# Down-projection weights of a float32 SwiGLU trunk: the low half comes from an accumulating transfer instead of a subtraction

## The chip, the cores and the metric

The kernel runs on one core of a Trainium2 chip. The metric is device time in microseconds (us), the median of several executions; lower is better.

## The reference

The program is a two-layer decoder trunk on 512 tokens of 1024 features, in float32. Layer 0 has a causal pooling mixer, layer 1 a latent attention; each mixer stands between two half-step SwiGLU feed-forward networks (FFNs), so there are four FFNs. The change touches the last product of each FFN alone:

```python
D_MODEL, SEQ, D_FF, FFN_HALF = 1024, 512, 2816, 0.5

def swiglu(h, w_gate, w_up, w_down):
    return (jax.nn.silu(h @ w_gate) * (h @ w_up)) @ w_down
...
        h = rmsnorm(x, ffn1_norm[i])
        x = x + FFN_HALF * swiglu(h, ffn1_w_gate[i], ffn1_w_up[i], ffn1_w_down[i])
```

## The kernel before

TensorE (PE in the rows) does its products in a float32 form with a short mantissa (float32r). To keep float32 precision, every operand is split into a high and a low half, `hi + lo = value`, and each product takes three matmuls in `mm3`: high by high, high by low, low by high. Only the last of the three reads the weights' low half.

Activations are kept with features in the 128 partitions and the 512 tokens along the free axis. Weights come from HBM tile by tile. `load_w` allocates three buffers of 128 x 1024 from the pool `wp`: `raw`, `whi` and `wlo`, each a ring of three. SyncE's queue (SP) loads `raw`; ScalarE (ACT) writes `whi`, a copy rounded to float32r; VectorE (DVE) writes `wlo = raw - whi`. These two are `split`, lines 117 and 118. TensorE then reads both.

An FFN has 22 blocks of 128 hidden features. They are worked off in three parts, `THIRDS`, of 8, 8 and 6 blocks. In each part the gate and up products are made (by `product` and by the seven-product scheme in `Two`), SiLU and the product with the up half follow (`gated`, lines 287 and 291), and the result is split into halves. Then the part's share of the down projection is made: eight tiles of weights, m = 0 to 7, one for each 128 output features. A tile of the first two parts has 1024 columns, and of the third 768; it takes 24 or 18 matmuls of 512 columns. VectorE adds half of the result to the residual (line 479). In the third part, each finished residual tile is at once prepared for the next layer on ScalarE and VectorE (`nxt.add`: lines 120, 121, 178, 181, 182).

The order of instructions on each engine isn't that of the program text. The language's planner orders them by its own costs, so weights of the first down tiles are split before the last gate and up results are done. What the rings allow still binds: the halves of tile m + 3 can only be written when TensorE is through with tile m, because both lie in the same buffers of `whi` and `wlo`.

GpSimd (POOL) has no work in the FFNs. It works in the two mixers (lines 182, 494, 834, 838, 937, 946).

Of the kernel before, what the change touches and what calls it, by code (L numbers as in the profile page):

```python
# [53 lines left out]
def _bits(v, n):  # L54
    """v cut to n significant bits (float64)."""
    m, e = np.frexp(v)
    return float(np.ldexp(np.trunc(np.ldexp(m, n)), e - n))
# [12 lines left out]
def _wrapped(v):  # L70
    """v less the nearest multiple of 2 pi, for an integer v, in extended precision."""
    pi2 = np.longdouble("6.283185307179586476925286766559005768")
    v = np.longdouble(v)
    return float(v - np.rint(v / pi2) * pi2)
# [3 lines left out]
def trunk(ctx: ExitStack, tc: tile.TileContext, a: dict, out: bass.AP):  # L78
# [29 lines left out]
    def mm3(ps, w, x, first, last):  # L108
        """w, x: (hi, lo) pairs; the product's three parts, in one group."""
        mm(ps, w[0], x[0], first, False)  # L110
        mm(ps, w[0], x[1], False, False)
        mm(ps, w[1], x[0], False, last)

    def split(src, hi, lo, scale=None):
        """hi + lo = src * scale exactly as float32, each with 12 bits."""
        if scale is None:
            nc.scalar.activation(hi, src, AF.Copy)  # L117
            nc.vector.tensor_tensor(out=lo, in0=src, in1=hi.bitcast(F32), op=ALU.subtract)  # L118
        else:
            nc.scalar.activation(hi, src, AF.Copy, scale=scale)  # L120
            nc.vector.scalar_tensor_tensor(  # L121
                out=lo, in0=src, scalar=scale, in1=hi.bitcast(F32), op0=ALU.mult, op1=ALU.subtract
            )
# [8 lines left out]

    # ---- x, constants
    gains = cp.tile([P, NG], F32, name="gains")
# [4 lines left out]
    nc.vector.memset(ones, 1.0)  # L139
    # the copy's table, ahead of its use  # L140
    nc.scalar.activation(small(1, tag="mx", bufs=6), ones[:, 0:1], AF.Copy)

    # ---- 1/sqrt on [P, n]
    def rsqrt(v, n, out=None):
# [18 lines left out]

    # ---- x_j: its gained halves for the next layer, and its share of the sum of squares
    class Prep:
# [23 lines left out]
        def rstd(self):  # L189
            """[P, NT]: token t of tile i in partition t, column i."""  # L190
            ps = aux()
            for i in range(NT):
                mm(ps[:, i : i + 1], self.sq[:, i * P : (i + 1) * P], ones[:, 0:1], True, True)
            v = small(NT, tag="ms")
            nc.vector.tensor_scalar(v, ps[:, :NT], 1.0 / D, EPS, op0=ALU.mult, op1=ALU.add)
            return rsqrt(v, NT, tp.tile([P, NT], F32, tag="rstd", name="rstd", bufs=2))

        def rstd_rows(self, r):
            """[P, S]: the same in every partition, tokens along the free axis."""
            ps = aux()  # L200
# [8 lines left out]
    def opening(wg, wu, prep):  # L209
        """the first tile of gate and up, as x and the weights come in."""  # L210
        half = WC // 2
# [46 lines left out]
    def ffn_in(fp, wg, wu, wd, prep, nxt, first, final):  # L258
# [5 lines left out]
        def product(w, x, turned=False, then=None):  # L264
            """then, if given, comes before the last steps"""
            hi, lo = load_w(w, WC)
# [16 lines left out]
        def gated(zg, zu):  # L283
            """silu(zg) * zu in halves; zg in parts, the last in the tile that is written."""
            z = zg[-1][1]
# [9 lines left out]

        # The first tiles take x unscaled, and their products are scaled by the tokens' 1/rms.
        # The others take xn, x scaled first, and most of them the gate's tiles two at a time,
        # by seven products of halves (Winograd's form of Strassen's): xn in blocks of 512
        # features by 256 tokens, the weights in blocks of 512 features by 128 columns.
        # Tokens of one size keep these sums as good as float32's own.  # L300
        xn, ts, kept = [None] * KD, {}, []
# [4 lines left out]
        def normed(k):  # L306
            """tiles k and KH + k of xn in halves; both stay in float32 as well."""
            tag, dt = (("s", F32), ("s", F32), ("chi", F32R), ("clo", F32R))[k]
# [12 lines left out]
        def x_sums(k):  # L321
            """the four sums of xn's blocks, a (hi, lo) pair for each tile of 128 features."""
            b11, b12, b21, b22 = (kept[k][:, c * C : (c + 1) * C] for c in range(4))
# [11 lines left out]
        def w_sums(top, low):  # L335
            """the blocks of two weight tiles, and their four sums, as (hi, lo) pairs."""
            hw = WC // 2
# [26 lines left out]
        class Two:  # L364
            """two tiles of columns by seven products, in two steps"""

# [17 lines left out]
            def end(self):  # L384
                """for each tile the parts it lies in; all but the first are in one tile"""
                p, q, u, za, zb = self.p, self.q, self.u, self.za, self.zb
# [25 lines left out]
        for f0, f1 in THIRDS:  # L412
# [55 lines left out]
            for m in range(KD):  # L468
                hi, lo = load_w(wd[m][:, f0 * P : f1 * P], nf * P)
                # the last tile of all leaves in two parts  # L470
                nc_ = 2 if final and f1 == NFT and m == KD - 1 else 1
# [16 lines left out]
    def pool_layer(prep, nxt):  # L488
        """x += scale * (window mean - token) @ w, tokens pooled by a banded product."""
        with tc.tile_pool(name="pp", bufs=1) as pp:  # L490
# [37 lines left out]
            def pools(q, m):  # L528
# [3 lines left out]
                for i in range(NT):  # L532
                    # 256 columns at a time: the band's own, then or before it zeros
                    at = min(i, 2) * P
# [34 lines left out]

    # ---- rotary tables [P, NT, 64], tokens in partitions; gains taken in  # L570
    tabs = {}
# [81 lines left out]
    def mla_layer(prep, nxt):  # L653
        with tc.tile_pool(name="mp", bufs=1) as mp:
# [21 lines left out]
            def latent(m):  # L676
                """features in partitions, gained but not yet scaled by their rms."""
                hi, lo = load_w(a["w_in"][m], WC)
# [18 lines left out]

            # shared rotary key
            raw = wp.tile([P, WC], F32, tag="raw", name="raw")
# [5 lines left out]
            )  # L705
            # high parts give the first 64 rows, low parts the others
            pk = acc()
# [16 lines left out]
            def rotated(dst, src, tab, heads):  # L724
                """src, dst: [P, NT, heads, 64] views, may be the same."""
                t1, t2 = tab
# [26 lines left out]
            def latent_rms(e, n):  # L753
                """r / rms of a latent, and its square."""
                ps = aux()
# [12 lines left out]
            for m in range(KQ):  # L768
                latent(m)
            # the exponential's table, ahead of its use  # L770
            nc.scalar.activation(small(1, tag="mx", bufs=6), gqk, AF.Exp)
# [8 lines left out]

            # Generators that yield the matmuls they issued, in columns of 512, so that
            # one head's attention can be cut into another pair's projections.
            def rsqrt_of(ss, f2, more=None):
                """1 / rms over a head, from sums of squares [P, NT, 2] and their scale."""
                v = tp.tile([P, NT, 2], F32, tag="v8", name="v8", bufs=2)
# [9 lines left out]
            def project(c, got):  # L795
                """heads 2c, 2c + 1: q, k, v with tokens in partitions; q unscaled, k and v scaled."""
                qsb = mp.tile([P, NT, 2, DN + DR], F32, tag="qsb", name="qsb", bufs=2)
# [8 lines left out]
                for i in range(NT):  # L806
# [18 lines left out]
                    yield 6.0  # L825
                # k's head norm, taken into k
                y = rsqrt_of(ss[:, 1], be2, skp)
# [43 lines left out]

                # q's rotary part, and its head norm for the scores' rows
                qpe = mp.tile([P, NT, 2, 2, DR], F32, tag="qpe", name="qpe")
# [10 lines left out]
            class Head:  # L884
                """one head's attention in steps; o, features in partitions, as (hi, lo)."""

# [11 lines left out]
                def turn_rot(self):  # L898
                    """[hi; lo] of q against k's hi and lo, each twice over."""
                    h = self.h  # L900
# [41 lines left out]
                def turn_p(self, half):  # L942
                    """P transposed: blocks of 128 keys by 256 queries, two to a slot."""
                    pts = [[slot([P, 2, 2 * P]) for _ in range(half + 1)] for _ in range(2)]
# [45 lines left out]

            # steps of the heads in turn, other products between them
            n = H // 2
# [76 lines left out]

# ---- layout on the host  # L1070


def _cols(v):
    """[n * P] -> [P, n]."""
    return v.reshape(-1, P).T


def _lhs(w):
    """[.., K, M] -> [.., M / P, P, K] : tile m, row p of each K block, K block by column."""
    *b, k, m = w.shape  # L1080
# [73 lines left out]
```

## Time and profile before

| | |
|---|---|
| time of the kernel before, 3 runs | 1698.12, 1699.06 (median), 1699.32 us |
| profiled execution: span from first to last instruction | 1697.1 us |
| TensorE busy in the span | 1683.8 us |
| VectorE busy | 1076.1 us |
| ScalarE busy | 702.3 us |
| GpSimd busy | 70.1 us |
| loads of the down projection | 64 of 512 KB and 32 of 384 KB |

The profiled execution has no run time of its own beside the span; the median of the three runs is 2.0 us above the span, which is what lies before the first and after the last instruction. TensorE's busy time counts an instruction from its first column in to its last column out, and these overlap from one matmul to the next; a pause of TensorE shows only where even the overlap is gone.

### The profile page before, as it was taken

The numbers are of one execution on the slowest core, as the hardware profiler recorded it, in microseconds if no ns is written. First come the engines' busy times: TensorE is split into PE (matmuls) and PEld (weight loads), VectorE is DVE, ScalarE is ACT, GpSimd is POOL, SyncE is SP. The second block draws the span as 40 slices with busy tenths as digits, with TensorE's granted clock in tenths as the row PEclk, the third lists the DMA queues.
The fourth block names the chain that finished last, engine by engine and source line by source line (L and its number), as shares of the span: only waits on it lengthen the run. The fifth ranks groups of instructions, "written<-read, shape, count | busy, mean of one in ns | idle before, by whom it ended". The sixth has DMA issues, their size and how long they took to land.

```text
span 1697.1 us, 23211 instructions
## 1 busy us (share of the span) xinstructions
PE 1683.8 (99%) x9238; PEld 1462.2 (86%) x9238; DVE 1076.1 (63%) x1824; ACT 702.3 (41%) x1163; POOL 70.1 (4%) x147
## 2 busy tenths in 40 slices
PE   8999999999999999999999999999999999999999
PEld 7888988887888988888889889888888789898897
DVE  8845645698845545569556455646778796465463
ACT  6423423364423423444324223546665453243241
POOL 0000000012000000000000000003321300000000
PEclk9999999999999999999999999999999999999999
DMA  5333332232322332332323323321112123233232
GB/s 176 97 109 97 104 98 97 87 114 76 111 92 95 106 98 96 90 109 88 112 98 102 99 99 89 103 90 52 44 57 88 63 87 106 93 100 106 94 94 93
DMA packets 48204, 161.54 MB, mean 95 GB/s; under 512 B 5728, under 2 KB 6496, under 8 KB 48096
## 3 DMA queue, kind: packets, MB, share of 16 engines
q1 hardware_dynamic: 47520, 159.34, 29.3%
q8 instruction: 72, 1.18, 0.3%
q10 hardware_dynamic: 576, 0.72, 0.1%
q14 instruction: 36, 0.29, 0.1%
HBM read 157.94 MB, written 2.10 MB: 94 GB/s over the span
## 4 chain that ended last, share of the span: by engine, by line
PE 97%; DVE 1%; ACT 0%; issue 0%; DMA 0%; POOL 0%; ACTq 0%; DVEq 0%; POOLq 0%
PE acc L106 95%; PE aux L670 1%; PE aux L106 1%; DVE slot L121 1%; PE aux L951 1%; DVE x L986 0%; DVE wlo L118 0%; DMA gains<-in_gains 0%; DMA pos_i<-in_pos 0%; ACT work L932 0%; DVE x L544 0%; POOL work L937 0%; ACT slot L117 0%; ACT slot L120 0%; ACT whi L117 0%
## 5 line engine op out<-in xcount | busy, mean ns | idle before, releaser
L106 PE MATMUL acc<-slot,whi 128*128 128x512 f32 x3212 | 994.1, 391 | 8.7 <-ACT whi L117 5.2
L106 PEld LDWEIGHTS acc<-slot,whi 128*128 128x128 f32 x3212 | 598.0, 189 | 132.3 <-DVE slot L121 5.5
L106 PE MATMUL acc<-slot,wlo 128*128 128x512 f32 x1598 | 622.2, 390 | 0.0
L117 ACT ACTIVATE whi<-raw 128x1024 fp32r<-128x1024 f32 (+2 forms) x237 | 239.5, 1013 | 526.6 <-PE acc L106 469.2
L118 DVE TENSOR_TENSOR wlo<-raw,whi 128x1024 fp32r<-128x1024 f32 (+2 forms) x236 | 276.4, 1173 | 152.8 <-ACT whi L117 150.9
L106 PEld LDWEIGHTS acc<-slot,wlo 128*128 128x128 f32 x1598 | 300.9, 188 | 63.3 <-DVE wlo L118 1.3
L106 PE MATMUL acc<-slot,hi 128*128 128x256 f32 x1296 | 239.4, 281 | 0.0
L106 PEld LDWEIGHTS acc<-slot,hi 128*128 128x128 f32 x1296 | 204.6, 190 | 5.9
L106 PE MATMUL acc<-slot,lo 128*128 128x256 f32 x648 | 182.4, 281 | 0.0
L479 DVE SCALAR_TENSOR_TENSOR x<-acc,x 128x512 f32<-128x512 f32 (+1 forms) x97 | 66.4, 684 | 169.3 <-PE acc L106 169.3
L117 ACT ACTIVATE hi<-s 128x1024 fp32r<-128x1024 f32 x72 | 76.0, 1060 | 154.7 <-DVE s L350 103.1
L106 PE MATMUL acc<-t,hi 128*128 128x256 f32 x720 | 136.4, 282 | 0.0
L106 PEld LDWEIGHTS acc<-slot,lo 128*128 128x128 f32 x648 | 122.9, 190 | 0.0
L395 DVE TENSOR_TENSOR work<-acc,work 128x256 f32<-128x256 f32 x180 | 72.7, 420 | 64.8 <-ACT work L379 33.1
L106 PEld LDWEIGHTS acc<-t,hi 128*128 128x128 f32 x720 | 110.8, 189 | 0.0
L118 DVE TENSOR_TENSOR lo<-s,hi 128x1024 fp32r<-128x1024 f32 x72 | 87.8, 1224 | 34.3 <-ACT hi L117 33.7
L106 PE MATMUL acc<-t,lo 128*128 128x256 f32 x360 | 101.7, 282 | 0.0
L350 DVE TENSOR_TENSOR s<-raw 128x512 f32<-128x512 f32 x72 | 49.2, 687 | 71.1 <-DMA raw<-in_ffn_gate 71.1
L106 PE MATMUL acc<-whi,slot 128*128 128x384 f32 (+2 forms) x320 | 87.7, 344 | 0.0
L117 ACT ACTIVATE slot<-work 128x512 fp32r<-128x512 f32 x104 | 62.1, 626 | 57.2 <-DVE work L291 50.1
L118 DVE TENSOR_TENSOR slot<-work,slot 128x512 fp32r<-128x512 f32 x104 | 68.8, 687 | 25.1 <-ACT slot L117 25.0
L287 ACT ACTIVATE work<-work 128x512 f32<-128x512 f32 x88 | 43.9, 537 | 59.7 <-DVE work L395 56.6
(184 smaller groups left out, 1478.4 us busy)
## 6 DMA issues: line engine op xcount, KB each, us to landing
raw<-in_ffn_gate SPq DMA_DIRECT2D x87, 512.0 KB, 3.4
raw<-in_ffn_up SPq DMA_DIRECT2D x87, 512.0 KB, 3.4
raw<-in_ffn_down SPq DMA_DIRECT2D x64, 512.0 KB, 3.5
raw<-in_ffn_down SPq DMA_DIRECT2D x32, 384.0 KB, 3.1
raw<-in_w_q SPq DMA_DIRECT2D x12, 384.0 KB, 3.0
raw<-in_w_in SPq DMA_DIRECT2D x8, 512.0 KB, 3.4
raw<-in_w_out SPq DMA_DIRECT2D x8, 512.0 KB, 3.4
x<-in_xT SPq DMA_DIRECT2D x8, 256.0 KB, 5.2
```

The costliest lines, as they stand in the source:

```text
L106: nc.tensor.matmul(ps, lhsT, rhs, start=start, stop=stop, skip_group_check=skip)
L117: nc.scalar.activation(hi, src, AF.Copy)
L118: nc.vector.tensor_tensor(out=lo, in0=src, in1=hi.bitcast(F32), op=ALU.subtract)
L121: nc.vector.scalar_tensor_tensor(out=lo, in0=src, scalar=scale, in1=hi.bitcast(F32), op0=ALU.mult, op1=ALU.subtract)
L287: nc.scalar.activation(z[:, cs], g[:, cs] if g is z else g, AF.Silu)
L350: nc.vector.tensor_tensor(out=out, in0=x, in1=y, op=op)
L395: nc.vector.tensor_tensor(out=out, in0=x, in1=y, op=ALU.add)
L479: nc.vector.scalar_tensor_tensor(out=xs[m][:, cs], in0=p[:, cs], scalar=0.5, in1=xs[m][:, cs], op0=ALU.mult, op1=ALU.add,)
L670: nc.tensor.transpose(p[:, i * P : (i + 1) * P], src(i), ident)
L951: nc.tensor.transpose(p[:, js], self.pr[i][:, js], ident)
```

## The change

The 96 loads of the down projection go through a new function. The raw tile is loaded as before. ScalarE then writes the negated, rounded copy into the low half's buffer. GpSimd issues a second transfer of the same weights from HBM, which is added onto that buffer, so that it holds `raw - round(raw)`. ScalarE makes the high half by a second pass over the raw tile. VectorE has no part in it any more. All other loads keep `load_w`. (The diff also takes comments and docstrings out, with line numbers kept or shifted by eleven.)

```diff
+    def load_w_added(src, cols):
+
+        raw = wp.tile([P, WC], F32, tag="raw", name="raw")
+        hi = wp.tile([P, WC], F32R, tag="whi", name="whi")
+        lo = wp.tile([P, WC], F32R, tag="wlo", name="wlo")
+        nc.sync.dma_start(raw[:, :cols], src)
+        nc.scalar.activation(lo[:, :cols], raw[:, :cols], AF.Copy, scale=-1.0)
+        nc.gpsimd.dma_start(lo[:, :cols], src, accum_op=ALU.add)
+        nc.scalar.activation(hi[:, :cols], raw[:, :cols], AF.Copy)
+        return hi, lo
...
             for m in range(KD):
-                hi, lo = load_w(wd[m][:, f0 * P : f1 * P], nf * P)
+                hi, lo = load_w_added(wd[m][:, f0 * P : f1 * P], nf * P)
```

## Rows read from the trace of the kernel before

**Rows 1.** The page: span and busy time of each engine.

```profile
span 1697.1 us, 23211 instructions
PE 1683.8 (99%) x9238; PEld 1462.2 (86%) x9238; DVE 1076.1 (63%) x1824; ACT 702.3 (41%) x1163; POOL 70.1 (4%) x147
```

**Rows 2.** Busy time in chosen stretches: two whole FFNs, and part of one's end.

```profile
core 0: us, PE busy (x) PEld busy (x) DVE busy (x) ACT busy (x) POOL busy (x), PEclk, DMA share, GB/s
390.00:750.00 360.00, 360.00 (x1957) 312.66 (x1955) 219.92 (x318) 137.09 (x187) 3.15 (x3) 1.00 0.31 98
...
334.00:340.00 6.00, 5.97 (x26) 4.82 (x27) 5.90 (x14) 3.92 (x6) 0.00 (x0) 1.00 0.23 66
```

**Rows 3.** The chain that ended last: start, length, what; one FFN's piece.

```profile
403.10 346.21 PE acc L106 x1883
```

**Rows 4.** Timeline of a first part: ScalarE's high copies, first reads of low halves.

```profile
101.05 1.06 ACT L117 ACTIVATE whi<-raw 128x1024 fp32r<-128x1024 f32 x1 [1.63 <-PE acc L106]
101.53 0.39 PE L106 MATMUL acc<-slot,wlo 128*128 128x512 f32 x1
...
112.41 0.39 PE L106 MATMUL acc<-slot,wlo 128*128 128x512 f32 x1
```

**Rows 5.** Timeline of a third part: the same pairs for m = 1 and m = 3.

```profile
325.00 0.85 ACT L117 ACTIVATE whi<-raw 128x768 fp32r<-128x768 f32 x1 [4.53 <-PE acc L106]
...
333.42 0.39 PE L106 MATMUL acc<-slot,wlo 128*128 128x512 f32 x1
...
335.30 0.85 ACT L117 ACTIVATE whi<-raw 128x768 fp32r<-128x768 f32 x1 [2.22 <-PE acc L106]
...
342.62 0.39 PE L106 MATMUL acc<-slot,wlo 128*128 128x512 f32 x1
...
346.27 0.85 ACT L117 ACTIVATE whi<-raw 128x768 fp32r<-128x768 f32 x1 [1.84 <-issue]
...
354.86 0.39 PE L106 MATMUL acc<-slot,wlo 128*128 128x512 f32 x1
```

**Rows 6.** Groups by line and shape: the high copies and the subtractions.

```profile
L117 ACT ACTIVATE whi<-raw 128x1024 fp32r<-128x1024 f32 x188 | 199.1, 1061 | 451.8 <-PE acc L106 408.4 <-issue 43.0 <-ACT slot L120 0.5
L117 ACT ACTIVATE whi<-raw 128x768 fp32r<-128x768 f32 x44 | 37.5, 852 | 72.1 <-PE acc L106 60.8 <-issue 11.3
L118 DVE TENSOR_TENSOR wlo<-raw,whi 128x1024 fp32r<-128x1024 f32 x188 | 231.8, 1234 | 130.3 <-ACT whi L117 128.5
L118 DVE TENSOR_TENSOR wlo<-raw,whi 128x768 fp32r<-128x768 f32 x44 | 42.0, 955 | 21.9 <-ACT whi L117 21.9
```

**Rows 7.** The page: SyncE's queue, and the down loads with time to landing.

```profile
q1 hardware_dynamic: 47520, 159.34, 29.3%
...
raw<-in_ffn_down SPq DMA_DIRECT2D x64, 512.0 KB, 3.5
raw<-in_ffn_down SPq DMA_DIRECT2D x32, 384.0 KB, 3.1
```

**Rows 8.** GpSimd: its shortest and longest usual instruction, and its longest waits.

```profile
L1143 POOL MEMSET const-bfloat16-1.0<- 128x1 bf16 x1 | 0.1, 102 | 0.0
L182 POOL TENSOR_TENSOR sqacc<-sqacc,work 128x512 f32<-128x512 f32 x14 | 22.4, 1601 | 35.9 <-ACT work L181 35.1
...
POOL kn L834 <- ACT work L865: 759.9, 1, 759.9
POOL band L494 <- ACT slot L120: 355.9, 1, 355.9
```

**Rows 9.** Timeline of ScalarE where the gate products end and down tiles begin.

```profile
91.44 1.06 ACT L117 ACTIVATE whi<-raw 128x1024 fp32r<-128x1024 f32 x1 [1.74 <-PE acc L106]
92.88 1.06 ACT L117 ACTIVATE whi<-raw 128x1024 fp32r<-128x1024 f32 x1 [0.38 <-PE acc L106]
93.84 0.37 ACT L287 ACTIVATE work<-acc 128x256 f32<-128x256 f32 x1
96.28 0.94 ACT L287 ACTIVATE work<-work 128x512 f32<-128x512 f32 x2 [2.08 <-DVE work L395]
```

## The prediction, made before the change was run

> **What bounds the kernel now.** I read the page's busy rows first, then stretches, then the chain of waits, then the timeline of the down stages. TensorE is busy for 1683.8 of 1697.1 us [rows 1]. So it pauses for 13.3 us in all, and the reader should look for where these lie: the stretch from 390 to 750 us, which holds a whole FFN and parts of its neighbours, has TensorE busy for 360.00 of 360.00 us at a granted clock of 1.00 [rows 2], and in the chain that ended last an FFN is one unbroken piece of TensorE, 346.21 us long [rows 3]. VectorE works 219.92 of these 360 us and ScalarE 137.09 [rows 2]: both have slack, and neither sets the end. Work taken from VectorE in an FFN buys nothing; the only question is whether the new route delivers the low half in time.
>
> How much time there is can be read from the timeline. In a first part ScalarE's high copy for tile m = 3 starts when the buffer comes free, at 101.05 us. The first low halves of m = 1 and m = 3 are read at 101.53 and 112.41, so a tile takes TensorE 10.88 / 2 = 5.44 us [rows 4], and one of 768 columns 18/24 of that, 4.08. From the copy's start TensorE still has two tiles to do; the low half is read from the third matmul of a tile on.
>
> **What is removed.** 96 subtractions on VectorE: 64 of 1.234 us and 32 of 0.955 us [rows 6, 7], 79.0 + 30.6 = 109.6 us of VectorE. Value: nothing, since TensorE doesn't wait in that stretch [rows 2].
>
> **What is added on ScalarE.** A second pass for each tile, bounded on both sides by the copy of the same shape, 1.061 and 0.852 us [rows 6]: 64 x 1.061 + 32 x 0.852 = 95.2 us. The negation comes first, so the high half is one pass later. For m = 3 of a third part the copy would end at 335.30 + 2 x 0.85 = 337.00, and the tile begins two matmuls before 342.62, about 342.2 [rows 5]: hidden by over 5 us. What is queued behind the two passes matters at one place, where the gate products end. There m = 1 and m = 2 are split at 91.44 and 92.88, a part of SiLU follows at 93.84, and the last SiLU pair at 96.28 after 2.08 us of idle time [rows 9]. With four passes instead of two: 91.44 + 4 x 1.06 = 95.68, plus the 0.37 us SiLU, 96.05. It just fits ahead of 96.28, with 0.2 us to spare. I cost it at nothing; without that cover it is one pass for each of the twelve stages, 8 x 1.06 + 4 x 0.85 = 11.9 us.
>
> **What is added as a transfer.** Call L the time from the negation's end to the low half's landing. No row of this trace shows an accumulating transfer or one issued by GpSimd, so I bound L.
> - From below: a plain load of the same tile, 3.5 us for 512 KB and 3.1 us for 384 KB [rows 7].
> - What one more operand costs: the queue's packets took 29.3% of 1697.1 us, 497 us, for 159.34 MB [rows 7]: 320 GB/s, so 1.64 us for 512 KB and 1.23 us for 384 KB. The transfer must read the buffer that it adds onto besides the weights, so I count two operands.
> - GpSimd's part in issuing: its instructions take from 0.10 to 1.60 us [rows 8]; I take 1.0, between the two.
> - From above: weights, old value and result each take a whole landing one behind another, 1.0 + 3 x 3.5 = 11.5 us and 1.0 + 3 x 3.1 = 10.3 us.
>
> My value is 3.5 + 1.64 + 1.0 = 6.1 us and 3.1 + 1.23 + 1.0 = 5.3 us. I lean to the lower end because everything but the extra operand is the known load.
>
> The Trainium skill (Collectives: The Full Stack, The bandwidth ceiling) says that an add inside the transfer engines costs no cycles of its own, only the second source read that halves the rate; no run so far shows it. By it the sum is the one above.
>
> **The windows for L.** In a first or second part m = 3's negation would end at 101.05 + 1.06 = 102.11, and its low half is read at 112.41 [rows 4]: 10.3 us. For m = 1 it would end at 91.44 + 1.06 = 92.50 [rows 9] against 101.53 [rows 4]: 9.0 us. In a third part, m = 1: 325.85 against 333.42, 7.6 us; m = 3: 336.15 against 342.62, 6.5 us, the tightest, because m = 0 and m = 1 are interleaved there and m = 0 frees its buffer late; m = 6: 347.12 against 354.86, 7.7 us [rows 5]. So 6.1 of at least 9.0 us, and 5.3 of at least 6.5 us. The transfers also have to keep pace: two operands are 3.3 us of all engines per 5.44 us tile, beside the plain load's 1.64. That is 4.9 us, under the 5.44 but close.
>
> **Queues.** SyncE's loads don't wait longer: a raw buffer is free after two ScalarE passes (2.12 us) instead of a copy and a subtraction (1.06 + 1.23 us). On GpSimd each transfer waits for a negation, and whatever stands behind it waits too; but in the FFNs nothing does. Its next work after the pooling stage waits 759.9 us for the attention's input, and the one memset before it waits 355.9 us for the first FFN's end [rows 8]. Had that memset been put ahead of the last transfers, they would be late once, by a few us.
>
> The sum: 0 on TensorE. The profiled execution's span stays at 1697.1 us, and with the 2.0 us around it the time is 1699, the median of before.
>
> **The rivals.**
> - *Transfers too slow (slower).* If an accumulating transfer takes the engines as long as four operands, 6.56 us for 512 KB and 4.92 us for 384 KB, it needs more than a tile's 5.44 and 4.08 us. L is then 1.0 + 1.86 + 6.56 = 9.4 us and 1.0 + 1.87 + 4.92 = 7.8 us, where 1.86 and 1.87 are the landing less its one operand. Per stage of 1024 columns m = 3 lands with 0.9 us to spare, m = 4 is 0.2 us late, m = 5 to 7 lose 1.1 us each: 3.5 x 8 stages = 28 us. Per stage of 768 columns m = 3 is 1.3 us late and four more lose 0.84 us: 4.7 x 4 = 19 us. In all 47 us, 1746. It decides from some three operands on; slower still, it grows by the full excess per tile. For it: nothing here shows the rate of such transfers. Against it: DMA share is 0.31 now [rows 2]. Chance 0.22.
> - *Landing too late (slower).* At the upper bound of 11.5 and 10.3 us, m = 3 and m = 6 wait in each stage: 2 x 1.2 x 8 = 19 us, and (3.8 + 2.6) x 4 = 26 us: 1744. It decides from L = 6.5 us in the third parts. Chance 0.12.
> - *ScalarE's passes ahead of SiLU (slower).* The 11.9 us above: 1711. The 0.2 us to spare speaks for it, VectorE's lighter load against it. Chance 0.09.
> - *GpSimd held up by VectorE (slower).* In a third part VectorE is busy for 5.90 of 6.00 us around m = 3's negation [rows 2]. If GpSimd can issue only when VectorE pauses, from 336.15 to about 340 us, L is 5.3 + 3.9 = 9.2 us, 2.7 us late, at most 4 x 2.7 = 11 us: 1710. The Trainium skill (SBUF — State Buffer, SBUF: two separate sides) states such a lock for transfers issued by GpSimd, 620 ns stretched to 3100 ns, but only beside VectorE's two-port modes, and says that two-input operations like those here keep clear of it; no run so far shows either. Chance 0.05.
> - *Faster.* The planner orders anew, and some of the 13.3 us of pauses outside the FFNs goes. At most a few us: 1695. Chance 0.05.
>
> **How the numbers follow.** No change has 0.47 and is the likeliest single case: 1699, with its own range 1696 to 1702. A measurement of this kernel tells about 0.2% (3.4 us) from nothing. The slower cases sum to 0.48, the faster one to 0.05. The range, 1695 to 1752, takes in every rival at its worked price; left out are about 0.02 below and about 0.12 above, where the transfers are slower than four operands.
>
> **What would show it.** Right: 96 transfers by GpSimd landing in 5 to 7 us; VectorE near 1076 - 110 = 966 us and ScalarE near 702 + 95 = 797 us; HBM reads up by 64 x 0.524 + 32 x 0.393 = 46 MB; no TensorE pause ended by `wlo`. Wrong: TensorE's idle time in the down stages ended by the transfer into `wlo`, first at m = 3 of a third part; landings that lengthen along a stage would be the rate, constant long ones the latency; SiLU starting later than the DVE result that feeds it would be ScalarE's passes.

## The result, and the profile of the kernel after

The changed kernel takes 1714.83 us (median of three runs, 1712.67 to 1716.84) against 1699.06: a ratio of 1.0092, with a 95% interval from 1.0074 to 1.0110. It is slower by 15.8 us, where no change was forecast. The profiled execution took 1716.84 us, with a span of 1715.1, 18.0 us above the 1697.1 of [rows 1]. (1.7 us lie outside the span here; the 2.0 that I had put there came from two different executions.)

First the page of the kernel after: span, busy times, the two queues that carry weights (packets, MB, share of 16 engines' span), and the loads of the down projection with their median time from issue to landing.

```profile
span 1715.1 us, 23473 instructions
PE 1690.3 (99%) x9238; PEld 1464.4 (85%) x9238; DVE 969.9 (57%) x1728; ACT 782.2 (46%) x1259; POOL 152.7 (9%) x243
...
q1 hardware_dynamic: 47520, 159.34, 30.0%
q0 software_dynamic: 13824, 46.14, 15.1%
...
raw<-in_ffn_down SPq DMA_DIRECT2D x64, 512.0 KB, 3.9
wlo<-in_ffn_down POOLq DMA_DIRECT2D x64, 512.0 KB, 7.7
raw<-in_ffn_down SPq DMA_DIRECT2D x32, 384.0 KB, 3.3
wlo<-in_ffn_down POOLq DMA_DIRECT2D x32, 384.0 KB, 6.4
```

VectorE lost 106 us of work and ScalarE gained 80, and neither shows in the time. The 18.0 us are TensorE's, in two parts. Span less busy time was 1697.1 - 1683.8 = 13.3 us [rows 1] and is 24.8 now: 11.5 us more of pauses. And its busy time grew by 6.5 us for the same 9238 instructions; most of this is matmuls at a lower clock, as the last stretches of this section show. The low halves take 7.7 and 6.4 us to land, where the plain loads of [rows 7] take 3.5 and 3.1.

Where do the new pauses lie? All but one of 0.28 us in the third parts, and most of their time in that of the first FFN. The last matmuls of that FFN's statistics (`sqacc`, the sum of squares that the next normalisation needs), at 365.61 us before, now start at 376.89, as these two rows show (timeline of TensorE, before):

```profile
365.61 1.02 PE L106 MATMUL aux<-ones,sqacc 128*128 128x1 f32 x8
```

and after:

```profile
376.89 1.02 PE L106 MATMUL aux<-ones,sqacc 128*128 128x1 f32 x8
```

So 11.3 us of the 18.0 are lost by there, and most of the rest in the three later third parts. I take the simpler place first. This is the third part of the third FFN, tile m = 3, the pair of [rows 5] one mixer later (timeline of ScalarE, GpSimd and TensorE; in brackets the idle time before, and what ended it):

```profile
1078.77 0.85 ACT L141 ACTIVATE whi<-raw 128x768 fp32r<-128x768 f32 x1 [1.47 <-PE acc L106]
1079.52 0.83 ACT L139 ACTIVATE wlo<-raw 128x768 fp32r<-128x768 f32 x1
...
1080.64 0.86 POOL L140 DMA_DIRECT2D wlo<-in_ffn_down  x1 [7.25 <-ACT wlo L139]
...
1087.01 0.50 PE L106 MATMUL acc<-slot,wlo 128*128 128x512 f32 x1 [0.78 <-DMA wlo<-in_ffn_down]
```

The high copy (line 141) runs first and the negation (line 139) second, the reverse of the program's text. The negation ends at 1080.35, GpSimd issues 0.29 us later, and the half lands at 1087.01: L is 6.66 us. TensorE wanted it at 1087.01 - 0.78 = 1086.23, that is 5.88 us after the negation. The second FFN's third part has pauses that end on `wlo` at m = 1 and m = 3 (1.12 and 0.27 us), and so has the last FFN's (0.95 and 1.16 us). The landings don't lengthen along a stage: the medians of the four third parts lie between 5.9 and 7.1 us for every m, with 6.1 for m = 0 and 6.0 for m = 7.

The first FFN's end has more in it. First the tables for the attention's rotation, which are loaded there (timeline of VectorE and TensorE):

```profile
336.24 0.17 DVE L597 CAST pos<-pos_i 128x4 f32<-128x4 int32 x1 [3.90 <-DMA pos_i<-in_pos]
...
336.94 0.69 DVE L118 TENSOR_TENSOR slot<-work,slot 128x512 fp32r<-128x512 f32 x1
...
337.68 0.69 DVE L118 TENSOR_TENSOR slot<-work,slot 128x512 fp32r<-128x512 f32 x1
...
337.68 0.79 PE L106 MATMUL acc<-slot,whi 128*128 128x512 f32 x1 [3.66 <-DVE slot L118]
```

VectorE stands 3.90 us before a conversion of 512 integers, whose load hasn't landed; the low half of the last hidden block stands behind it; TensorE stands 3.66 us for that. Nothing here is a weight. The loads that are late, in the list of DMA issues of the kernel before:

```profile
braw<-in_band ACTq DMA_DIRECT2D x1, 576.0 KB, 3.7
...
pos_i<-in_pos SPq DMA_DIRECT2D x1, 2.0 KB, 2.9
```

and after:

```profile
braw<-in_band ACTq DMA_DIRECT2D x1, 576.0 KB, 8.3
...
pos_i<-in_pos SPq DMA_DIRECT2D x1, 2.0 KB, 6.3
```

Next, 20 us later, the pooling mixer's band (`braw` as loaded, `band` as copied), its scale factors `psc`, and the low half of m = 6 (timeline of GpSimd, VectorE, ScalarE and TensorE):

```profile
354.95 3.64 DVE L511 TENSOR_SCALAR psc<-gains 128x2 f32<-128x2 f32 x4
...
355.01 0.86 POOL L140 DMA_DIRECT2D wlo<-in_ffn_down  x1 [3.50 <-ACT wlo L139]
355.55 3.01 POOL L505 MEMSET band<- 128x3072 f32 x1
...
363.37 1.16 ACT L506 ACTIVATE band<-braw 128x1152 fp32r<-128x1152 f32 x1 [2.70 <-DMA braw<-in_band]
...
364.49 0.79 PE L106 MATMUL acc<-slot,wlo 128*128 128x512 f32 x1 [2.83 <-DMA wlo<-in_ffn_down]
```

This low half takes 9.5 us from issue to use, against 6.4 in the median. Busy time in stretches of the same end (columns as in [rows 2]) shows what these pauses bring behind them:

```profile
326.00:334.00 8.00, 8.00 (x51) 6.86 (x50) 2.04 (x4) 4.93 (x9) 1.72 (x2) 1.00 0.81 177
...
337.70:341.00 3.30, 3.30 (x8) 2.62 (x9) 2.34 (x9) 1.21 (x2) 0.00 (x0) 0.50 0.00 0
341.00:345.00 4.00, 4.00 (x14) 3.13 (x13) 2.09 (x8) 1.81 (x4) 0.86 (x1) 0.65 0.63 145
...
350.00:361.60 11.60, 11.60 (x52) 9.33 (x50) 9.72 (x26) 7.43 (x13) 5.23 (x4) 1.00 0.92 220
...
364.50:368.00 3.50, 3.50 (x9) 2.78 (x10) 2.49 (x3) 2.11 (x4) 0.00 (x0) 0.55 0.43 133
```

Behind each of the two long pauses the granted clock is 0.50 to 0.65, the lower of the two levels (1.2 GHz) for most of it, with TensorE fully busy. That costs 3.3 x 0.50 + 4.0 x 0.35 + 3.5 x 0.45 = 4.6 us of the 6.5; the rest isn't placed. And the DMA share is 0.81 and 0.92 in the stretches in which the late loads are under way.

### The profile page after: what moved, and what is told of

The parts are those of the page before. It is cut to its first block, busy times and chain, and to the rows that moved or that the text cites. A ratio compares the mean times of both kernels' runs of the same rounds, so it can differ in the third digit from the quotient of the medians.

```text
span 1715.1 us, 23473 instructions
## 1 busy us (share of the span) xinstructions
PE 1690.3 (99%) x9238; PEld 1464.4 (85%) x9238; DVE 969.9 (57%) x1728; ACT 782.2 (46%) x1259; POOL 152.7 (9%) x243
## 3 DMA queue, kind: packets, MB, share of 16 engines
q0 software_dynamic: 13824, 46.14, 15.1%
## 4 chain that ended last, share of the span: by engine, by line
PE 71%; issue 23%; DMA 3%; DVE 2%; POOL 1%; ACT 1%; POOLq 0%; SPq 0%; ACTq 0%; DVEq 0%
PE acc L106 69%; DMA wlo<-in_ffn_down 3%; POOL wlo L140 1%; PE aux L681 1%; PE aux L106 1%; DVE slot L121 1%; PE aux L962 1%; DVE wlo L118 0%; DVE x L997 0%; DMA raw<-in_ffn_gate 0%; ACT work L943 0%; DVE x L555 0%; POOL work L948 0%; ACT work L831 0%; ACT slot L117 0%
## 5 line engine op out<-in xcount | busy, mean ns | idle before, releaser
L117 ACT ACTIVATE whi<-raw 128x1024 fp32r<-128x1024 f32 (+2 forms) x141 | 144.3, 1027 | 231.7 <-PE acc L106 181.6
L118 DVE TENSOR_TENSOR wlo<-raw,whi 128x1024 fp32r<-128x1024 f32 (+2 forms) x140 | 167.5, 1199 | 104.1 <-ACT whi L117 102.9
L140 POOL DMA_DIRECT2D wlo<-in_ffn_down x96 | 83.2, 867 | 1309.6 <-ACT wlo L139 1240.5
L141 ACT ACTIVATE whi<-raw 128x1024 fp32r<-128x1024 f32 (+1 forms) x96 | 94.9, 989 | 216.5 <-PE acc L106 147.5
L139 ACT ACTIVATE wlo<-raw 128x1024 fp32r<-128x1024 f32 (+1 forms) x96 | 93.3, 972 | 1.3 <-PE acc L106 1.3
```

The costliest lines, as they stand in the source:

```text
L139: nc.scalar.activation(lo[:, :cols], raw[:, :cols], AF.Copy, scale=-1.0)
L140: nc.gpsimd.dma_start(lo[:, :cols], src, accum_op=ALU.add)
L141: nc.scalar.activation(hi[:, :cols], raw[:, :cols], AF.Copy)
```

## The experiments

My theory after this reading: the time goes to (T1) low halves that land later than their window in the third parts, because L is longer and the window shorter than I had them, and (T2) loads of other work at the first FFN's end that the new transfers slow down. The rivals were the transfers' rate, ScalarE's passes or the planner's new order, and GpSimd and VectorE in each other's way. The ratios are against the kernel before, on the same chip. Its medians there lie between 1698.6 and 1698.8 us, so times of different kernels are set side by side too; each has only 4 to 11 executions, which spread by up to 7 us.

**Is it the third parts?** The first kernel takes them back to the subtraction, the other 64 tiles staying with the transfer; the second only the first FFN's.

```diff
-                hi, lo = load_w_added(wd[m][:, f0 * P : f1 * P], nf * P)
+                hi, lo = (load_w if f1 == NFT else load_w_added)(wd[m][:, f0 * P : f1 * P], nf * P)  # first kernel
+                hi, lo = (load_w if first and f1 == NFT else load_w_added)(wd[m][:, f0 * P : f1 * P], nf * P)  # second
```

> The 32 tiles of 384 KB (third parts) go back to the subtraction, the 64 of 512 KB keep the accumulating transfer. Theory W (the low half lands later than its window in the third parts, and at the first FFN's end the transfers hold up the loads for the position tables): all of that lies in third parts, so the time falls to 1699 to 1701 us. Rival R (accumulating transfers as a stream are too slow for the engines): two thirds of the bytes stay, so at least 10 of the 15.8 us stay, 1709 us or more. Rival A (ScalarE's added passes and the order that the planner gives them): two thirds of the passes stay, about 1709 us.

Measured: 1700.75 us, ratio 1.0012 [1.0003, 1.0022]. Two pauses on `wlo` remain, 0.93 and 0.37 us. The pause of 0.93 us is in a first part, so not all of it lies in third parts. Of the loss of 15.8 us, some 14 hang on these 32 of 96 tiles. A rate too slow, and ScalarE's passes, would have shown in the other 64 as well.

> Only the eight tiles of the first FFN's third part go back to the subtraction; the other 88 keep the accumulating transfer. Theory W puts about 11 us of the loss there (pauses of 3.66 and 2.84 us, about 4.5 us at half clock behind them, and little else): 1703 to 1705 us. If the loss were even over the four third parts: 1710 us or more.

Measured: 1707.15 us, 1.0047 [1.0032, 1.0062]: 7.7 us gained, which is less than the 11.3 that the profiled execution loses there, and a time between the two that I had named. Eight pauses of 0.29 to 0.96 us on `wlo` stay, one of them in the first FFN's first part, the others in the later FFNs. By medians, half of the loss is at the first FFN's end.

**Do the passes, the order or VectorE's relief matter by themselves?** The transfer is left out, so the low half is the bare negated high half; all else stays.

```diff
-        nc.gpsimd.dma_start(lo[:, :cols], src, accum_op=ALU.add)
```

> The accumulating transfer is left out: the low half's buffer holds the negated high half, and the products are not the reference's. ScalarE's passes stay, and VectorE has no subtraction. Theory W: no landing to wait for, no transfers ahead of the tables: 1698 to 1700 us, as before the change. Rival A (the passes and the planner's order cost): 1704 us or more.

Measured: 1699.16 us, 1.0001 [0.9992, 1.0011]. Its page:

```profile
span 1697.4 us, 23164 instructions
...
PE 1683.9 (99%) x9238; PEld 1462.3 (86%) x9238; DVE 969.7 (57%) x1728; ACT 783.5 (46%) x1259; POOL 69.8 (4%) x147
```

VectorE's 106 us less and ScalarE's 81 us more, in the order that the planner gave this kernel, change nothing. The loss comes with the transfers. The small loads are quick again too: 2.5 us for the 2 KB and 4.6 for the 576 KB, instead of 6.3 and 8.3.

**What does the addition cost a transfer?** The same transfer by GpSimd without the addition (the low half then holds the raw weights).

```diff
-        nc.gpsimd.dma_start(lo[:, :cols], src, accum_op=ALU.add)
+        nc.gpsimd.dma_start(lo[:, :cols], src)
```

> The second transfer is a plain one (no addition), so the low half's buffer holds the whole weight and the products are not the reference's; ScalarE's passes, GpSimd's issue and the bytes from HBM are the same. Theory W with the length in the software route: landing falls only by the operand that is not read, 7.7 to about 6.4 us and 6.4 to about 5.4 us, and the time to 1702 to 1707 us. Theory W with the length in the addition itself: landing falls to about 4.8 and 4.2 us (SyncE's 3.9 and 3.3 plus 0.9 of issue), and the time to 1699 to 1701 us. Rival A: the passes are still there, 1713 to 1715 us.

Measured: 1701.50 us, 1.0018 [1.0008, 1.0027]. Its queue and its landings, as on the page above:

```profile
q0 software_dynamic: 13824, 46.14, 7.8%
...
wlo<-in_ffn_down POOLq DMA_DIRECT2D x64, 512.0 KB, 4.6
wlo<-in_ffn_down POOLq DMA_DIRECT2D x32, 384.0 KB, 4.1
```

So being issued by GpSimd costs 4.6 - 3.5 = 1.1 us and 4.1 - 3.1 = 1.0 us over the loads of [rows 7] (0.9 us over SyncE's loads of the same run, which took 3.7 and 3.2), and the addition 7.7 - 4.6 = 3.1 us and 6.4 - 4.1 = 2.3 us on top. The engines are held 1.95 times as long: 15.1% of 1715.1 us is 259 us, 7.8% of this run's span of 1701.9 is 133 us, for the same 46.14 MB. The Trainium skill (Collectives: The Full Stack, The bandwidth ceiling) says that the add itself costs no cycles and the second source read halves the rate: the engines' time agrees with that. The landing doesn't follow from it: 259 - 133 = 126 us over 46.14 MB is 1.4 us for 512 KB, less than half of the 3.1 us. The plain kernel still loses 2.9 us: its tables' load, 5.3 us long, holds up VectorE too, and TensorE pauses 2.69 us for it at 333.02.

**Negation first.** The planner's order of the two passes is turned round; nothing else changes.

```diff
-        nc.scalar.activation(lo[:, :cols], raw[:, :cols], AF.Copy, scale=-1.0)
+        neg = nc.scalar.activation(lo[:, :cols], raw[:, :cols], AF.Copy, scale=-1.0)
...
-        nc.scalar.activation(hi[:, :cols], raw[:, :cols], AF.Copy)
+        with tc.issue_after(neg.ins):
+            nc.scalar.activation(hi[:, :cols], raw[:, :cols], AF.Copy)
```

> An ordering edge makes ScalarE write the negation before the high copy in every down tile (the planner had put the high copy first). Theory W: each accumulating transfer starts 0.8 to 1.0 us sooner, so the pauses of 0.3 to 1.2 us at m = 1 and m = 3 of the third parts shrink to 0 to 0.4 us, in all 3 to 4 us: about 1711 us, with the first FFN's end as it was. Rival R: the stream is bound by its rate, no gain, 1714 to 1715 us. Rival A: the high half comes later and is waited for, 1715 us or more.

Measured: 1709.68 us, 1.0067 [1.0052, 1.0082]. Of the pauses on `wlo` in the later FFNs one is left, 0.69 us. The first FFN's end keeps both of its long ones, 3.98 us behind the tables and 2.16 us on `wlo`. The order was worth 5.15 us by medians. In the profiled executions the pauses on `wlo`, other than the one at the first FFN's end, went from 4.56 to 0.69 us; what the rest is, the traces don't settle, because the clock behind the long pauses also differs between the two.

**Half transfers.** Two accumulating transfers for each tile, one behind the other.

```diff
-        nc.gpsimd.dma_start(lo[:, :cols], src, accum_op=ALU.add)
+        for c in (slice(0, cols // 2), slice(cols // 2, cols)):
+            nc.gpsimd.dma_start(lo[:, c], src[:, c], accum_op=ALU.add)
```

> The accumulating transfer goes in two halves of the columns, the first ones needed first; all else as in the changed kernel. In the plain form the landing was 4.6 us for 512 KB and 4.1 us for 384 KB, so the addition costs 3.1 and 2.3 us, about 6 ns per KB. If that cost goes with the bytes, the first half of 256 KB lands about 5.2 us after its issue, 2.5 us sooner than the whole, and the pauses on the low half in the later FFNs go; the tables are still late: 1707 to 1711 us. If it is a fixed cost of any accumulating transfer, the half lands at about 6.7 us, two of them hold each other up, and the time is 1714 us or more.

Measured: 1706.78 us, 1.0042 [1.0025, 1.0059]. The median landing over both halves is 6.3 us (256 KB) or 5.8 us (192 KB). By itself the first half takes 5.7 or 5.3 us, the second 6.7 or 6.2: half of the bytes saved 2.0 us of 7.7 and 1.1 of 6.4. How much of L is fixed this doesn't show, since the second half moves beside the first. The first columns come in time, and the pauses in the later FFNs are gone or below 0.25 us; the first FFN's end keeps 4.47 us behind the tables and 2.13 us on `wlo`.

**The tables.** Their three loads are moved to the kernel's start, into buffers of their own.

```diff
+        for t, n in zip(tables, ("pos", "freq", "rope_gains")):
+            nc.sync.dma_start(t, a[n])
...
-            pos_i = rp.tile([P, NT], I32, name="pos_i")
-            nc.sync.dma_start(pos_i, a["pos"])
...
+            pos_i, freq, hg = tables
...
```

> The three small loads for the position tables are issued at the kernel's start instead of at the first FFN's end; nothing else. Theory W: TensorE's pause of 3.66 us near 334 us goes, and with it the stretch at half clock behind it (about 3 us), so 1714.8 - 6.4 = about 1708 us; the pause near 362 us may stay. Rivals R and A: VectorE's wait for that load is only where a late stage shows, another wait takes its place, 1714 to 1715 us.

Measured: 1711.26 us, 1.0074 [1.0058, 1.0089]. The 3.66 us pause and the low clock behind it are gone, but the low halves that were hidden by that pause are late now: 1.19, 0.55 and 1.66 us on `wlo` in the same stage. 3.6 us came back of the some 6.7 that the pause and its clock had cost (3.66 + 3.3 x 0.50 + 4.0 x 0.35). Both edits together:

> The early tables and the negation first, together. Theory W: the pause behind the tables is gone and the windows are one pass wider; what is left is m = 1, 3 and 6 at the first FFN's end (1.2, 0.6 and 1.7 us with early tables alone, each about 0.8 us smaller) and a part of it in the last FFNs: 1702 to 1706 us. If the two repairs don't add up (rival: a pause only moves to the next late buffer), 1708 us or more.

Measured: 1707.04 us, 1.0042 [1.0027, 1.0057]. One long pause is left, m = 6 of the first FFN, 2.20 us on `wlo` at 359.21.

**Is m = 6 the pooling stage's doing?** One kernel holds the band's load back behind the last negation, another moves GpSimd's memset of the band to VectorE; both have the tables early, so 1711.26 us is what they stand against.

```diff
...
-            nc.scalar.dma_start(braw, a["band"])
+            with tc.issue_after(negs[-1]):
+                nc.scalar.dma_start(braw, a["band"])          # first kernel
...
-            nc.gpsimd.memset(band.rearrange("p v g t -> p (v g t)").bitcast(F32), 0.0)
+            nc.vector.memset(band.rearrange("p v g t -> p (v g t)").bitcast(F32), 0.0)   # second
```

> Early tables, and an ordering edge that holds the pooling stage's 576 KB load back until ScalarE has negated m = 7 of the first FFN's third part. With early tables alone TensorE paused 1.67 us for m = 6 there, while the transfer engines were 93% busy. If loads that share the engines lengthen that landing, the pause falls to 0 to 0.7 us and the time by 1 to 2 us, 1709 to 1710 us. If it is GpSimd's memset or the window alone, the pause stays at 1.5 us or more.

Measured: 1709.47 us, 1.0065 [1.0047, 1.0084]. The pause at m = 6 falls to 0.26 us, as it should if the band's load made that half late; but the next one, at m = 7, is 1.85 us: the collision moved. The band's load still takes 8.3 us. The time itself lies within the spread of the kernel with early tables alone (1707.51 to 1714.27).

> Early tables, and the pooling stage's memset of 3072 columns moved from GpSimd to VectorE, so that it doesn't stand between the transfers of m = 6 and m = 7. In the changed kernel four tiny VectorE operations took 3.64 us beside that memset on GpSimd. If the memset is what makes m = 6 late there, the pause of 1.67 us falls under 0.7 us and the time by 1 to 2 us; if not, it stays, and the tiny operations take their 0.6 us again: 1710 to 1712 us.

Measured: 1709.58 us, 1.0068 [1.0052, 1.0085]. A pause of 1.46 us on `wlo` stays at 356.91: the memset isn't what makes that half late. But the four small instructions on `psc`, 3.64 us beside GpSimd's memset, are back at 0.36 (timeline of VectorE):

```profile
350.75 2.62 DVE L507 MEMSET band<- 128x3072 f32 x1 [0.71 <-DVE t2k L656]
...
355.03 0.36 DVE L513 TENSOR_SCALAR psc<-gains 128x2 f32<-128x2 f32 x4
```

**All low halves in time.** A fourth buffer for the low half, room for which comes from one activation slot and one work tile; tables early.

```diff
-        lo = wp.tile([P, WC], F32R, tag="wlo", name="wlo")
+        lo = wp.tile([P, WC], F32R, tag="wlo", name="wlo", bufs=4)
...
```

> Early tables, and a fourth buffer in the ring of low halves, paid for with one activation slot (39 to 38) and one work tile (7 to 6); accumulating transfers in all 96 tiles, high copy first as the planner had it. Theory W: the negation of tile m + 4 instead of m + 3 waits for tile m, so the window grows by a tile's 4.1 to 5.4 us and all pauses on the low half go: 1699 to 1702 us. Rival R: the stream's rate binds, buffers don't help, 1707 us or more.

Measured: 1702.76 us, 1.0019 [1.0010, 1.0029]. No pause on `wlo` is left anywhere; one of 1.01 us ends on `sqacc` at 365.85. With negation first and the band's load held back besides:

> Early tables, negation first, four buffers of low halves (with one slot and one work tile fewer) and the pooling stage's load held back; accumulating transfers in all 96 tiles. Theory W: no pause on a low half is left and the pooling stage isn't held up: 1698 to 1701 us, level with the kernel before, not under it, since VectorE's free time buys TensorE nothing. If some rate of the transfers still costs: 1702 us or more.

Measured: 1702.68 us, 1.0022 [1.0012, 1.0031]. Again no pause on `wlo`, but one of 1.31 us on `sqacc` at 365.20, with a low clock behind it. I first took the memset for its cause and moved it to VectorE as well. (The text on record that follows says that this kernel has the first block by subtraction; what it has is the fourth buffer.)

> The kernel with all repairs (negation written first, tables loaded early, the first feed-forward block's third part by subtraction), and beside them the memset of band moved from GpSimd to VectorE. With all repairs alone the time was 1702.68 us, 3.6 us above the kernel before, and what stood in its profile was four small VectorE instructions on psc that took 3.63 us beside GpSimd's memset, and a pause of 1.31 us of TensorE that ended on sqacc, with the half clock behind it. If that memset is what is left: 1698.5 to 1701 us, and the pause that ended on sqacc is gone. If something else is left (transfers that share the DMA engines with loads, at the first block's end above all): 1702 to 1703.5 us, and a pause stands there under another name.

Measured: 1705.94 us, 1.0044 [1.0027, 1.0060]: slower, not faster. That guess fell. Its trace shows what had stood behind both (timeline of ScalarE, VectorE and TensorE):

```profile
349.90 0.85 ACT L145 ACTIVATE whi<-raw 128x768 fp32r<-128x768 f32 x1 [1.09 <-PE acc L106]
...
356.74 1.17 ACT L515 ACTIVATE band<-braw 128x1152 fp32r<-128x1152 f32 x1 [5.99 <-DMA braw<-in_band]
...
358.55 0.75 DVE L121 SCALAR_TENSOR_TENSOR slot<-x,gains,slot 128x512 fp32r<-128x512 f32 x1 [5.33 <-ACT slot L120]
...
368.38 1.84 PE L106 MATMUL aux<-ones,sqacc 128*128 128x1 f32 x8 [3.18 <-DVE sqacc L197]
```

ScalarE stands 5.99 us before the copy of the band (3.50 us in the kernel with all repairs, 3.19 with early tables and four buffers), because the band's load takes over 8 us; the residual's halves and squares stand behind it, VectorE waits for these, and TensorE for VectorE. It is the tables' case once more, on another engine. So the copy was given to GpSimd, which has nothing else to do there (negation first, tables early and four buffers kept; the band's load where it was):

```diff
-            nc.scalar.activation(band[:, :, :, P : P + BW], braw, AF.Copy)
+            nc.gpsimd.tensor_copy(band[:, :, :, P : P + BW], braw)
```

> Negation written first, tables loaded early, four low buffers, and the copy of the pooling band from braw moved from ScalarE to GpSimd, which has nothing else to do there. (A correction to the expectation of the kernel with all repairs and the memset on VectorE: what both of these hold is the fourth low buffer, not a first block by subtraction.) Theory: what is left after the repairs is ScalarE standing in order before that copy, 3.2 to 6.0 us, until the band's load, slowed by the accumulating transfers from 3.7 to over 8 us, has landed; the square of the residual tile stands behind it, then VectorE's sum, then TensorE. By it: 1699 to 1701 us, no wait of ScalarE on braw and no pause on sqacc with the half clock behind it. Rival, VectorE held by GpSimd (its memset, and now a copy more): 1702.5 to 1704 us, and the pause on sqacc stays or grows.

Measured: 1700.83 us, 1.0013 [1.0005, 1.0022], and 1699.23 us in the profiled execution, whose span of 1697.4 us is close to the 1697.1 of before (the end of the next section says why that flatters it). Between 13.1 and 386.7 us TensorE doesn't pause for as much as 0.1 us. The band's load is as late as ever, but it is GpSimd that stands for it (its timeline; the interval of the time overlaps those of the two kernels at 1702.7 us, but the pause on `sqacc` is gone):

```profile
355.95 1.68 POOL L511 CAST band<-braw 128x1152 fp32r<-128x1152 f32 x1 [4.78 <-DMA braw<-in_band]
```

The same edit without the fourth buffer:

> As the kernel with tables early and negation first (1707.04 us), with the band's copy on GpSimd and no fourth low buffer. Theory: the low half's own lateness at m = 6 stays (a pause of 2.20 us there with half the clock behind it), the wait on the band goes: 1704 to 1707 us. If the band's copy alone had been the cause of the pauses there: 1700 to 1702 us.

Measured: 1710.57 us, 1.0067 [1.0054, 1.0081], 3.5 us slower than without that edit, which neither side had expected. Here the planner put the last low half behind the copy on GpSimd (timeline of GpSimd and TensorE):

```profile
357.71 1.38 POOL L509 CAST band<-braw 128x1152 fp32r<-128x1152 f32 x1 [5.31 <-DMA braw<-in_band]
359.05 0.86 POOL L140 DMA_DIRECT2D wlo<-in_ffn_down  x1
...
365.01 0.80 PE L106 MATMUL acc<-slot,wlo 128*128 128x512 f32 x1 [5.85 <-DMA wlo<-in_ffn_down]
```

Whichever engine stands for the slowed load, what is queued behind it is late: VectorE with the tables, ScalarE with the band, GpSimd with the next transfer.

## Why the prediction was wrong

**What held.** TensorE sets the end, and VectorE's relief is worth nothing (1699.16 us without the transfers, at 970 us of VectorE). ScalarE's second pass cost no time, and 80 us of its work rather than 95, mostly since a pass overlaps those beside it (one starts at 1079.52, 0.10 us before 1078.77 + 0.85). The transfers' rate isn't the bound: 259 us for 46.14 MB is 2.94 us for 512 KB, less than the 3.3 us that I had counted for two operands, and landings don't lengthen along a stage, which I had named as the rate's sign. But transfers and loads fill the engines in a third part (DMA share 0.97, 0.80 and 0.94 in the three stretches of 4 us from 1086 to 1098), and how much of L comes from sharing them no run separates. The issue by GpSimd was worth 0.9 to 1.1 us against my 1.0. And the place that I named as the tightest, m = 3 of a third part, is where low halves came late, with m = 1 beside it. (The stretch of 360 us in [rows 2] holds one whole FFN, as the prediction says, and not two, as the line above the rows has it.)

**What failed.** The likeliest case rested on "6.1 of at least 9.0 us, and 5.3 of at least 6.5 us". Both sides of that were off.
- *L, the term for the extra operand.* I took a transfer's time of one operand, 1.64 and 1.23 us. The addition cost 3.1 and 2.3 us of landing, nearer to a second landing. With the hop of 0.3 us from the negation to the issue, L is 8.0 and 6.7 us instead of 6.1 and 5.3. I had chosen the low end of my bounds because everything but the operand was known; the operand was the one unknown, and it carried the verdict.
- *The windows.* "The negation comes first" is the program's order; the planner put the high copy first in 87 of the 96 tiles, m = 1 and m = 3 of every stage among them, and their windows were shorter by a pass of 0.85 or 1.06 us. For m = 3 of a third part that makes 6.5 - 0.85 = 5.65 us, and 5.88 was measured against an L of 6.66. In the longer parts m = 1 has 9.0 - 1.06 = 7.9 us against 8.0: it is only just late, once by 0.28 us. Negation first brought 5.15 us back.
- *"SyncE's loads don't wait longer."* I looked at the buffers that they wait for and not at the DMA engines that they share. A load of 2 KB went from 2.9 to 6.3 us and one of 576 KB from 3.7 to 8.3, and each held up an engine in whose order other work stood. At the first FFN's end this, with m = 6 behind it, is most of the 11.3 us. The early tables gave 3.6 us back; the band's copy on GpSimd gave 1.9 us by medians whose intervals overlap, and 0.8 us between two profiled executions without a stretch at the lower clock (spans of 1698.2 with early tables and four buffers, and 1697.4).
- *Nothing for the clock.* I priced a late half at its lateness. Some 4.6 of the 18.0 us are TensorE at the lower clock behind pauses.
- *The memset,* dismissed as "late once, by a few us": its effect on the transfers was nothing that the runs could show, but VectorE finished nothing beside it for 3 us.

Of the rivals, "landing too late" is the one that happened, for which I had 0.12 and 1744 us. Its point of decision, L = 6.5 us in the third parts, was right. Its place was right in part: it had m = 3 and m = 6 late in every stage, and m = 1 and m = 3 of the third parts were, m = 6 only at the first FFN's end. Its price was that of its extreme, L = 10.3 us. With L at 6.7 us the later third parts lose about a microsecond each at m = 1 and m = 3. It needed no extreme to be true: with 1.2 us between my L and the window, one pass and one mis-sized term sufficed, and a case just past the point of decision had no price and no chance of its own. That 1714.83 lies inside the stated range, and near the 1711 and 1710 of two other rivals, is luck: ScalarE's passes cost nothing (1699.16 us with them and without the transfers), and GpSimd wasn't held up (0.29 us from negation to issue in 95 of 96 tiles).

What stays open: the best of these kernels is 2.1 us above the one before by medians (1700.83 to 1698.74). That its profiled execution, its fastest, comes close to the profiled one of before is luck with the clock. Both have a pause of 2.8 us in the attention, which ends near 1341.5 us and has nothing to do with the change. Behind it the kernel before ran at the lower clock for a while, and the best one didn't, as the clock of the same stretch shows, before:

```profile
1341.50:1345.00 3.50, 3.47 (x9) 2.62 (x10) 3.50 (x3) 0.00 (x0) 1.11 (x1) 0.59 0.38 130
```

and in the best kernel:

```profile
1341.50:1345.00 3.50, 2.73 (x11) 1.94 (x12) 3.42 (x3) 0.00 (x0) 1.01 (x1) 1.00 0.33 117
```

Four of its eleven executions have a mean granted clock of 1.000, with spans of 1697.4 to 1698.3 us; three of the fifteen of before have it, with 1696.0 to 1696.4. So 1.0 to 2.3 us stay lost where the clock takes no part, and I didn't see in a trace what takes them. No version beat the kernel before, and with VectorE off the path none had anything to gain.

## What to carry to other kernels

When an edit turns work of an engine with slack into a transfer, the question is whether the longest plausible landing fits the shortest window: take the window in the worst order that the planner may choose, and give the case "just past the window" a chance. Then look at every small load that shares the stage: ask which in-order engine will stand for it, and what stands behind that. A pause of TensorE is to be priced with the slower clock that may follow it, and two single profiled executions are to be compared only after a look at their clocks.

## What the runs showed of the hardware beyond that

- An accumulating transfer into SBUF from GpSimd's queue holds the engines 1.95 times as long as a plain one, and lands 3.1 us (512 KB) or 2.3 us (384 KB) later. Split in two, the first 256 KB land in 5.7 us, the second in 6.7, the whole in 7.7.
- GpSimd spends 0.87 us to issue one of them and 0.53 us for the plain one.
- VectorE's four scalings of a 128 x 2 tile took 3.64 us beside GpSimd's memset of 3.01 us, ending within 0.03 us of it (358.59 and 358.56), and 0.36 us with the memset on VectorE. The last of the four alone took 3.41 us of it (355.17 to 358.58), and the three VectorE instructions behind it ended at 358.59 as well. The Trainium skill (SBUF — State Buffer, SBUF: two separate sides) states that VectorE's two-port modes and GpSimd share a port that one of them holds for a whole instruction; these rows agree with it, though none says in which mode the scalings ran. The lock that I had priced, transfers waiting for VectorE, shows in no run.
- Behind the pauses of 3.66 and 2.83 us TensorE's granted clock stood at 0.50 and 0.55, while behind the one of 1.12 us, at 720.63, it stayed at 1.00. The length of the pause doesn't settle it: the pause of the attention, 2.78 to 2.83 us in all 17 profiled executions, was followed by a stretch at 0.50 in 11 of them and by full clock in 6, and one of 2.20 us brought the lower clock (early tables and negation first) where 2.16 us didn't (negation first).
